# The identity and eight transposes in the rounded 32-bit type, in a hybrid encoder layer

## The chip, the cores and the metric

The kernel runs on one core of a Trainium2 chip. The metric is the device time of one execution in microseconds (us); smaller is better. TensorE (PE) multiplies and transposes, VectorE (DVE), ScalarE (ACT) and GpSimd (POOL) do the rest, and SyncE (SP) issues most loads.

## The reference

One layer of a bidirectional encoder on 1024 tokens of 1024 features, in float32: a gated feed-forward half-step, a mixer of two attention branches, a second half-step and a last norm.

```
h = x + 0.5 * swiglu(rms_norm(x, n1), wg1, wu1, wd1)          # d_ff = 2816
u = rms_norm(h, nm)
qa, ka, va, qb, kb, vb, ga, gb = split(u @ w_in)
ya = neighbourhood_attention_2d(qa, ka, va, rpb)               # 8 heads of 64, 8x16 windows, bias
yb = windowed_gqa_sink(rope(qb), rope(kb), vb, sink)           # 8 query heads, 2 key/value heads,
                                                               # |i - j| <= 128, a sink logit
h = h + (sigmoid(ga) * (ya @ w_a) + sigmoid(gb) * (yb @ w_b)) @ w_out
h = h + 0.5 * swiglu(rms_norm(h, n2), wg2, wu2, wd2)
y = rms_norm(h, nf)
```

The change concerns `vb`, the values of branch B: 1024 tokens by 2 heads of 64.

## The kernel before, in words

All matrix products work on the "rounded" 32-bit type (`F32R` in the code, `fp32r` in the profile). An operand is split into a rounded high part and a low part that holds the rest, and each product is the sum of three matmuls: high by high, high by low, low by high (`mm3`, L149, L153, L155). The feed-forward products and the input projection are arranged as Strassen-like products of half matrices (P1 to P7).

The stages follow one another on TensorE: the first feed-forward half, a transition with the norm, the input projection (`products` with `store_z`), the two attention branches with gates and branch projections as filling work, the output projection, the second feed-forward half.

**The start.** `make_identity` fills `ident`, 128x128, on POOL with a memset (masks.py:197) and an affine select (masks.py:199). The first thing that TensorE does is `keep_busy(28)` (L914 to L919): 28 transposes of the identity whose result nobody reads. Behind them, in TensorE's queue, comes the first stage. Its order is written out by hand, token by token, in `LOADS` and `TABLE`, inside a block in which the order of all five queues is given by the program. `hi:` and `lo:` tokens make the two parts of an operand (L998 and L327 on ACT, L1000 and L334 on DVE), `square:` squares blocks of the input on ACT (L965), `add:` adds them on DVE (L968), `mm:` runs one step of a product, `sum:` adds the squares over the partitions with a matrix of ones (L974), `spread:` turns the resulting factors across the partitions with four transposes (L986), and the `y:` tokens (L1005) apply them. The identity is made outside that block, ahead of it in the program; outside such blocks a scheduler sets the place of an instruction in its engine's queue.

**The values of branch B.** The input projection writes chunk 17, the transposed values (128 features by 1024 tokens), to DRAM. `v_b` (L1153) loads it back to `mix["vr"]`, and `turn_v` (L1158) transposes it in eight blocks of 128x128 with the identity (L1163), four to a PSUM bank; then `split` (L95 on ACT, L98 on DVE) makes the high and low parts from PSUM. Both are hooked into the input projection and run among its products.

The identity also serves the transposes of the transitions (`turned`, L142), of the first stage's `spread` (L986) and of the attention probabilities (`turn`, L1620). The tile `gain` in the constant pool has one buffer, which holds one norm's gains after another, and the ones of the first stage (L926 to L929) before them.

Of the kernel before, what the change touches and what calls it, by code (L numbers as in the profile page):

```python
# [10 lines left out]
F32 = mybir.dt.float32  # L11
F32R = mybir.dt.float32r
# [3 lines left out]
P = 128  # L16
# [15 lines left out]
def f32v(ap):  # L32
    return ap.bitcast(F32)
# [3 lines left out]
def trunk_kernel(ctx, tc, x, xt, n1, wg1, wu1, wd1, nm, win, rpb, sink, wa, wb, wout,  # L37
                 n2, wg2, wu2, wd2, nf, c_rope, c_mask_a, c_mask_b, out):
    nc = tc.nc
# [7 lines left out]
    const = ctx.enter_context(tc.tile_pool(name="const", bufs=1))  # L47
    main = ctx.enter_context(tc.tile_pool(name="main", bufs=1))
# [5 lines left out]
    def nm_(s):  # L54
        uid[0] += 1
        return f"{s}_{uid[0]}"

    ident = const.tile([P, P], F32, name="ident")
    make_identity(nc, ident)
    nhalf4 = const.tile([P, 4], F32, name="nhalf")  # L60
    nc.gpsimd.memset(nhalf4, -0.5)
    nhalf = nhalf4[:, 0:1]
# [17 lines left out]
    def bank(tag):  # L80
        return ps.tile([P, 512], F32, tag=tag, name=nm_(tag))
# [4 lines left out]
    def xs4():  # L86
        return main.tile([P, 1024], F32, tag="xs", bufs=2, name=nm_("xs"))
# [4 lines left out]
    pin = tc.keep_in_program_order  # L92
# [44 lines left out]
    def turned(xs):  # L137
        pts = []
        for half in range(2):
            pt = bank("d")  # L140
            for c in range(4):
                nc.tensor.transpose(pt[:, c * P:(c + 1) * P], xs[:, (half * 4 + c) * P:(half * 4 + c + 1) * P], ident)  # L142
            pts.append(pt.rearrange("p (c t) -> p c t", c=4))
        return pts

# [45 lines left out]
    def rhs(o):  # L191
        return [ar[o][:, k:k + 2, :].rearrange("p a (b t) -> p (a b) t", b=2) for k in (0, 2)]
# [648 lines left out]
    for i in range(NC8 + 2 * len(gates)):  # L841
        n = int(95 - 1.3 * i)
# [71 lines left out]
    def keep_busy(n):  # L914

        b = bank("g")
        for i in range(n):
            k = i % 4 * P
            nc.tensor.transpose(b[:, k:k + P], ident, ident)  # L919

    def first_stage():
        load, _, _, _, pieces, (multiply, finish), hand_over, load_early = hg
# [9 lines left out]
        for token in LOADS.split():  # L932
# [10 lines left out]
            else:  # L943
                k = 2 * (t - 1) + a[1]
# [17 lines left out]
        def do(op, a):  # L962
            if op == "square":
                n, c = int(a[0]), int(a[1])
                nc.scalar.activation(sq[place[4 * (1 - n) + c]], block(c, 0, n), AF.Square, scale=D ** -0.5)  # L965
            elif op == "add":
                d, e = [sq[k] for k in sums[int(a[0])]]
                nc.vector.tensor_tensor(d, d, e, op=ALU.add)  # L968
            elif op == "sum":
                i = int(a[0])  # L970
                if i == 0:
                    mean.append(bank("g"))
                for k in range(4):
                    nc.tensor.matmul(mean[0][:, k * P:(k + 1) * P], sq[3 * i][:, k * P:(k + 1) * P], ones, start=i + k == 0, stop=i == 1,  # L974
                                     skip_group_check=True)
            elif op == "eps":
                i = int(a[0])
                nc.vector.tensor_scalar(st[i][1], st[1][0] if i else mean[0].rearrange("p (k c) -> p k c", c=P)[:, :, 0], EPS, None, op0=ALU.add)
            elif op == "pow":
                i = int(a[0])  # L980
                nc.gpsimd.tensor_tensor(st[i][0], st[i][1], nhalf4, op=ALU.pow)
            elif op == "spread":
                i = int(a[0])
                r[i] = bank("d" if i else "g")
                for k in range(4):
                    nc.tensor.transpose(r[i][:, k * P:(k + 1) * P], st[i][0][:, k:k + 1].to_broadcast([P, P]), ident)  # L986
            elif op == "stat":
                t = int(a[0])
                nc.scalar.activation(toks[:, t - 4], toks[:, t - 4], AF.Square, scale=D ** -0.5,
                                     accum_out=st[1][0][:, t - 4:t - 3])  # L990
            elif op == "keep":
                rms["row"] = main.tile([P, 512], F32, tag="s1", bufs=1, name=nm_("s1"))
                nc.scalar.copy(rms["row"], r[0])
            elif a[0] == "X":
                c = int(a[1])
                h, l = [v[:, c, :] for v in rhs(B21)]
                if op == "hi":
                    nc.scalar.activation(h, block(c, 0, 1), AF.Copy, scale=n1c[:, 4 + c:5 + c])  # L998
                else:
                    nc.vector.scalar_tensor_tensor(out=l, in0=block(c, 0, 1), scalar=n1c[:, 4 + c:5 + c], in1=f32v(h),  # L1000
                                                   op0=ALU.mult, op1=ALU.subtract)
            elif op == "y":
                n, h, c = int(a[0][0]) - 1, int(a[0][1]) - 1, int(a[1])
                d, k = block(c, h, n), 4 * n + c
                nc.vector.scalar_tensor_tensor(out=d, in0=d, scalar=n1c[:, k:k + 1],  # L1005
                                               in1=rms["row"] if (n, h) == (1, 0) else r[h], op0=ALU.mult, op1=ALU.mult)
            elif op == "t":
                c = int(a[1])
                y11, y21, y12, y22 = block(c, 0, 0), block(c, 0, 1), block(c, 1, 0), block(c, 1, 1)
                d, u, v = {"1": (y12, y12, y11), "2": (y22, y22, y12), "3": (y11, y22, y11), "4": (y21, y21, y22)}[a[0]]  # L1010
                nc.vector.tensor_tensor(d, u, v, op=ALU.subtract)
            elif a[0] in RIGHTS:
                c = int(a[1])
                src, g = block(c, *BLOCKS[a[0]]), RIGHTS[a[0]]
                if ar[g].dtype != F32R:
                    new_ar(g)
                h, l = [v[:, c, :] for v in rhs(RIGHTS[a[0]])]
                if op == "hi":
                    nc.scalar.copy(h, src)
                else:  # L1020
                    nc.vector.tensor_tensor(l, src, f32v(h), op=ALU.subtract)
            elif op == "load":
                i, m, half = [int(k) for k in a]
                load(i, m, half, {(0, 0): 4, (0, 1): 5, (1, 0): 6}[m, half])
            else:
                q = int(a[1]), a[0], int(a[2])
                if op == "mm":
                    if q not in mm:
                        mm[q] = multiply(*q)
                    drain(mm[q], 1)  # L1030
# [21 lines left out]
    z_d = dram.tile([GA, T], F32, name="z_d")  # L1052
# [8 lines left out]
    gain = load_gain(nm[0])  # L1061
    mix = {}
# [89 lines left out]

    def v_b():  # L1153
        mix["vb"] = [new_fx(k, F32R).rearrange("p (t d) -> p t d", t=NTT) for k in (0, 1)]
        mix["vr"] = xs4()
        pin(nc.sync.dma_start(mix["vr"], z_d[17 * P:18 * P, :]))

    def turn_v():  # L1158
        r = mix["vr"]
        for n in range(2):  # L1160
            pt = bank("g")
            for i in range(4):
                nc.tensor.transpose(pt[:, i * P:(i + 1) * P], r[:, (4 * n + i) * P:(4 * n + i + 1) * P], ident)  # L1163
            pt = pt.rearrange("p (b s d) -> p b s d", s=2, d=HD)
            for s in range(2):
                v = mix["vb"][s][:, 4 * n:4 * n + 4, :]
                split(v[:, :, :HD], v[:, :, HD:], pt[:, :, s, :])
# [77 lines left out]
    for c in range(5):  # L1245
        n = 14 * (NG - 1) - 6 - 7 * c
# [367 lines left out]
    def turn(un):  # L1614
        nk = un["nk"]
        un["p"] = [ws4()[:, :768].rearrange("p (k s t) -> p k s t", k=3, s=2) for _ in range(2)]
        for s in range(2):
            pt = bank("d")
            for i in range(nk):
                nc.tensor.transpose(pt[:, i * P:(i + 1) * P], un["pr"][s][:, i * P:(i + 1) * P], ident)  # L1620
# [183 lines left out]
    gain = load_gain(n2[0])  # L1804
# [13 lines left out]
    gain = load_gain(nf)  # L1818
# [122 lines left out]
```

## Time and profile before

| | |
|---|---|
| time, median of 3 runs | 1912.86 us (1912.05 to 1912.9) |
| the profiled execution's own time | 1912.05 us |
| its span | 1910.1 us |
| TensorE busy | 1901.1 us, 9020 instructions |
| VectorE, ScalarE, GpSimd busy | 1456.1, 961.3, 244.3 us |
| read from and written to HBM | 244.06 and 121.83 MB, 192 GB/s over the span |
| eight transposes of the values (L1163) | from 810.87 us, 272 ns each |
| 28 transposes of `keep_busy` (L919) | from 1.52 us, 421 ns each |

Rows of a timeline give the start and the length in us, the engine, the line, what is written and read, and in brackets the idle time ahead and what ended it. Matmuls are pipelined: one starts before the one ahead has ended, so the distance of two starts is their price in a stream, and the length of one is longer. Weight loads (PEld) run beside the matmuls.

### The profile page before, as it was taken

To read this page: it belongs to the slowest core of one execution; us is meant where nothing else is said; L and a number is where in the kernel's file an instruction comes from. 1 tells how busy PE (TensorE), PEld (TensorE's weight loads), DVE (VectorE), ACT (ScalarE), POOL (GpSimd) and SP (SyncE) were. 2 spreads that over 40 slices of the span, in tenths; PEclk is the share of its full clock that TensorE was granted. 3 is DMA by queue.
4 is the path that set the end of the run, shared out by engine and by line. 5 is a ranking of instruction groups with operands and counts; after the bars stand their busy time and mean duration, and the time that the engine had idled before them with its cause. 6 is when DMAs were issued, how large, how long until landed. Compare 5 with 4: busy or idle time off the path is not lost.

```text
span 1910.1 us, 26150 instructions
## 1 busy us (share of the span) xinstructions
PE 1901.1 (100%) x9020; PEld 1595.1 (84%) x9020; DVE 1456.1 (76%) x2644; ACT 961.3 (50%) x1876; POOL 244.3 (13%) x453
## 2 busy tenths in 40 slices
PE   9999999999999999999999999999999999999998
PEld 8888888888888888898898888888888888888886
DVE  8988888868957788666888999789665566559664
ACT  7533545544446543444898885274333333344453
POOL 0011232210000112211112300010010001000011
PEclk9999999999999999999999999999999999999999
DMA  7256977887454367855647969653333323492341
GB/s 270 95 188 217 336 273 289 298 293 282 127 166 135 112 206 225 243 192 206 181 123 207 296 227 335 232 195 132 136 111 107 108 89 111 162 357 93 110 139 61
DMA packets 176963, 365.84 MB, mean 192 GB/s; under 512 B 17728, under 2 KB 75968, under 8 KB 176832
## 3 DMA queue, kind: packets, MB, share of 16 engines
q1 hardware_dynamic: 136784, 236.23, 37.6%
q0 software_dynamic: 39184, 126.90, 19.2%
q8 instruction: 71, 1.16, 0.3%
q10 hardware_dynamic: 864, 1.05, 0.2%
q14 instruction: 60, 0.49, 0.1%
HBM read 244.06 MB, written 121.83 MB: 192 GB/s over the span
## 4 chain that ended last, share of the span: by engine, by line
PE 96%; ACT 2%; DVE 1%; DMA 0%; issue 0%; SPq 0%; POOLq 0%; POOL 0%; DVEq 0%
PE g L149 18%; PE g L155 18%; PE g L153 18%; PE d L155 12%; PE d L149 12%; PE d L153 12%; PE d L1620 2%; PE g L1634 1%; PE d L1596 1%; PE d L1597 1%; PE g L1639 1%; PE d L142 1%; ACT fa L1604 0%; ACT ws L95 0%; DMA fx<-in_xt_dram 0%; DVE ws L98 0%
## 5 line engine op out<-in xcount | busy, mean ns | idle before, releaser
L149 PE MATMUL g<-ar,ws 128*128 128x512 f32 x1062 | 407.0, 393 | 0.2
L153 PE MATMUL g<-ar,ws 128*128 128x512 f32 x1062 | 403.8, 390 | 0.0
L155 PE MATMUL g<-ar,ws 128*128 128x512 f32 x1062 | 402.6, 390 | 0.0
L149 PE MATMUL d<-ar,ws 128*128 128x512 f32 x706 | 275.3, 390 | 0.0
L155 PE MATMUL d<-ar,ws 128*128 128x512 f32 x706 | 274.9, 389 | 0.1
L153 PE MATMUL d<-ar,ws 128*128 128x512 f32 x706 | 274.8, 389 | 0.0
L155 PEld LDWEIGHTS g<-ar,ws 128*128 128x128 f32 x1062 | 199.2, 188 | 41.8
L153 PEld LDWEIGHTS g<-ar,ws 128*128 128x128 f32 x1062 | 199.4, 188 | 40.7
L149 PEld LDWEIGHTS g<-ar,ws 128*128 128x128 f32 x1062 | 196.4, 188 | 37.1 <-ACT xs L1331 1.1
L334 DVE TENSOR_TENSOR ws<-raw,ws 128x512 fp32r<-128x512 f32 x216 | 147.6, 689 | 78.5 <-ACT ws L327 77.7
L327 ACT CAST ws<-raw 128x512 fp32r<-128x512 f32 x216 | 132.7, 620 | 143.1 <-PE g L155 61.2
L155 PEld LDWEIGHTS d<-ar,ws 128*128 128x128 f32 x706 | 132.5, 188 | 28.0 <-DVE ws L334 0.5
L153 PEld LDWEIGHTS d<-ar,ws 128*128 128x128 f32 x706 | 132.6, 188 | 27.7 <-DVE ar L1000 0.3
L149 PEld LDWEIGHTS d<-ar,ws 128*128 128x128 f32 x706 | 132.7, 188 | 27.1
L95 ACT CAST ws<-raw 128x512 fp32r<-128x512 f32 x88 | 54.9, 623 | 115.5 <-PE d L155 63.6
L98 DVE TENSOR_TENSOR ws<-raw,ws 128x512 fp32r<-128x512 f32 x88 | 60.5, 688 | 55.2 <-ACT ws L95 55.1
L95 ACT CAST ar<-raw 128x512 fp32r<-128x512 f32 (+1 forms) x80 | 52.1, 654 | 84.4 <-PE g L153 51.5
L446 POOL DMA_DIRECT2D hid<-fx x91 | 49.5, 544 | 343.2 <-DVE fx L506 221.6
L149 PE MATMUL g<-ws,ws 128*128 128x512 f32 x232 | 90.9, 392 | 0.0
L153 PE MATMUL g<-ws,ws 128*128 128x512 f32 x232 | 90.3, 389 | 0.0
L155 PE MATMUL g<-ws,ws 128*128 128x512 f32 x232 | 90.1, 390 | 0.0
L95 ACT CAST ws<-ar 128x512 fp32r<-128x512 f32 x104 | 64.3, 618 | 47.4 <-PE g L155 25.4
(382 smaller groups left out, 3878.7 us busy)
## 6 DMA issues: line engine op xcount, KB each, us to landing
raw<-hid SPq DMA_DIRECT2D x70, 512.0 KB
hid<-fx POOLq DMA_DIRECT2D x91, 256.0 KB, 2.9
ar<-in_ffn_w_down_dram SPq DMA_DIRECT2D x32, 512.0 KB
raw<-in_ffn_w_up_dram SPq DMA_DIRECT2D x31, 512.0 KB
wo_d<-made POOLq DMA_DIRECT2D x28, 512.0 KB, 4.6
raw<-in_ffn_w_gate_dram SPq DMA_DIRECT2D x27, 512.0 KB
hid<-fa POOLq DMA_DIRECT2D x51, 256.0 KB, 2.9
ar<-zs_d POOLq DMA_DIRECT2D x48, 256.0 KB, 9.3
```

The lines of the kernel that those rows point to most:

```text
L95: hi = nc.scalar.copy(dst_hi, src)
L98: (eng or nc.vector).tensor_tensor(dst_lo, src, f32v(dst_hi), op=ALU.subtract)
L142: nc.tensor.transpose(pt[:, c * P:(c + 1) * P], xs[:, (half * 4 + c) * P:(half * 4 + c + 1) * P], ident)
L149: o = nc.tensor.matmul(b, lhs[0], r[0], start=first, stop=False, **kw)
L153: nc.tensor.matmul(b, lhs[0], r[1], start=False, stop=False, **kw)
L155: nc.tensor.matmul(b, lhs[1], r[0], start=False, stop=last, **kw)
L327: nc.scalar.copy(w[0][:, :512], a)
L334: nc.vector.tensor_tensor(w[0][:, 512:], a, f32v(w[0][:, :512]), op=ALU.subtract)
L446: nc.gpsimd.dma_start(hid[PRODUCTS.index(p), i], src)
L1596: nc.tensor.matmul(b[:, :nw], un["q"][s], un["kd"][s][:, k0 * P:k1 * P], start=True, stop=False)
L1597: nc.tensor.matmul(b[:, :nw], un["q"][s], un["kl"][s][:, k0 * P:k1 * P], start=False, stop=True)
L1620: nc.tensor.transpose(pt[:, i * P:(i + 1) * P], un["pr"][s][:, i * P:(i + 1) * P], ident)
```

## The change

`ident` becomes a tile of the rounded type. The plain identity is made in `plain`, a view of the one `gain` buffer, and a copy on VectorE writes `ident` from it. The eight transposes of `turn_v` take the values, the identity and the output as the rounded type; for that the values are loaded to a tile of this type, from the same ring of buffers as before. All other transposes read `ident` as plain 32-bit.

```diff
-    ident = const.tile([P, P], F32, name="ident")
-    make_identity(nc, ident)
+    ident = const.tile([P, P], F32R, name="ident")
+    plain = const.tile([P, 1152], F32, tag="gain", bufs=1, name="plain")[:, :P]
+    make_identity(nc, plain)
+    nc.vector.tensor_copy(ident, plain)
...
-            nc.tensor.transpose(b[:, k:k + P], ident, ident)
+            nc.tensor.transpose(b[:, k:k + P], f32v(ident), f32v(ident))
...
-        mix["vr"] = xs4()
-        pin(nc.sync.dma_start(mix["vr"], z_d[17 * P:18 * P, :]))
+        mix["vr"] = main.tile([P, 1024], F32R, tag="xs", bufs=2, name=nm_("vr"))
+        pin(nc.sync.dma_start(f32v(mix["vr"]), z_d[17 * P:18 * P, :]))
...
-                nc.tensor.transpose(pt[:, i * P:(i + 1) * P], r[:, (4 * n + i) * P:(4 * n + i + 1) * P], ident)
+                nc.tensor.transpose(pt[:, i * P:(i + 1) * P].bitcast(F32R), r[:, (4 * n + i) * P:(4 * n + i + 1) * P], ident)
```

The three other uses of the identity (L142, L986, L1620) get `f32v(ident)` in the same way. Behind the start every line number is 2 higher in the changed kernel.

How the queues stand, first VectorE's at the start of the program. The names are tiles (`ar`, `ws`, `xs`, `fx`, `raw` are work buffers, `n1c` the first norm's gains); in brackets are the engines whose signals an instruction waits for. Before:

```order
L1000 SCALAR_TENSOR_TENSOR ar_80<-fx_77,n1c,ar_80 128x512 [waits DMAHW1_49,DMAHW0_49,Activation_49]
L334 TENSOR_TENSOR ws_169<-raw_103,ws_169 128x512 [waits DMAHW2_49,Activation_49]
L1000 SCALAR_TENSOR_TENSOR ar_80<-fx_77,n1c,ar_80 128x512 [waits DMAHW3_49,Activation_49]
L968 TENSOR_TENSOR xs_133<-xs_133 128x512 [waits Activation_49]
L1000 SCALAR_TENSOR_TENSOR ar_80<-fx_78,n1c,ar_80 128x512 [waits DMAHW4_49,Activation_49]
L1000 SCALAR_TENSOR_TENSOR ar_80<-fx_78,n1c,ar_80 128x512 [waits Activation_49]
L334 TENSOR_TENSOR ws_188<-raw_107,ws_188 128x512 [waits DMAHW5_49,Activation_49]
```

And now:

```order
L1002 SCALAR_TENSOR_TENSOR ar_82<-fx_79,n1c,ar_82 128x512 [waits DMAHW1_49,DMAHW0_49,Activation_49]
L336 TENSOR_TENSOR ws_171<-raw_105,ws_171 128x512 [waits DMAHW2_49,Activation_49]
L1002 SCALAR_TENSOR_TENSOR ar_82<-fx_79,n1c,ar_82 128x512 [waits DMAHW3_49,Activation_49]
L970 TENSOR_TENSOR xs_135<-xs_135 128x512 [waits Activation_49]
L1002 SCALAR_TENSOR_TENSOR ar_82<-fx_80,n1c,ar_82 128x512 [waits DMAHW4_49,Activation_49]
L1002 SCALAR_TENSOR_TENSOR ar_82<-fx_80,n1c,ar_82 128x512 [waits Activation_49]
L61 CAST ident<-plain 128x128 [waits Pool_49]
L336 TENSOR_TENSOR ws_190<-raw_109,ws_190 128x512 [waits DMAHW5_49,Activation_49]
```

The copy of the identity (L61) stands in the seventh place, behind six instructions of the first stage. TensorE's queue at the start, before:

```order
L919 MATMUL g_139<-ident 128x128 [waits Pool_49]
L919 MATMUL g_139<-ident 128x128 x27
L149 MATMUL d_175<-ar_80,ws_169 128x512 [waits Activation_49]
L153 MATMUL d_175<-ar_80,ws_169 128x512 [waits DVE_49]
L155 MATMUL d_175<-ar_80,ws_169 128x512 [waits DVE_49]
```

And now:

```order
L921 MATMUL g_141<-ident 128x128 [waits DVE_49]
L921 MATMUL g_141<-ident 128x128 x27
L151 MATMUL d_177<-ar_82,ws_171 128x512 [waits Activation_49]
L155 MATMUL d_177<-ar_82,ws_171 128x512
L157 MATMUL d_177<-ar_82,ws_171 128x512
```

The first of the 28 transposes waits for VectorE and no longer for POOL; the place of the 28 is the same. On POOL the filling of the ones (L931) now stands behind the affine select and waits for VectorE. The last place is ScalarE's queue around the eight transposes, where `g` are the banks of the turned values, `fx` their high parts and `ws` weights of later products. Before:

```order
L324 CAST ws_6778<-fx_77 128x4x128
L324 CAST ws_6778<-raw_6487 128x4x128
L95 CAST fx_6579<-g_6759 128x4x64
L95 CAST v_6755<-fa 128x8x64
L95 CAST fx_6579<-g_6768 128x4x64
L95 CAST fx_6580<-g_6759 128x4x64
L95 CAST fx_6580<-g_6768 128x4x64
L1116 ACTIVATE fa<-d_6785 128x512
```

And now:

```order
L326 CAST ws_6780<-fx_79 128x4x128
L97 CAST fx_6581<-g_6761 128x4x64
L326 CAST ws_6780<-raw_6489 128x4x128
L97 CAST v_6757<-fa 128x8x64
L97 CAST fx_6581<-g_6770 128x4x64
L97 CAST fx_6582<-g_6761 128x4x64
L1118 ACTIVATE fa<-d_6787 128x512
L97 CAST fx_6582<-g_6770 128x4x64
```

The first copy of turned values moved one place up, the last one place down; VectorE's subtractions that go with them move likewise. Elsewhere all queues stand as before.

More of the change, by code (lines that the diff above doesn't have):

```diff
@@ L141, in turned @@
             for c in range(4):
-                nc.tensor.transpose(pt[:, c * P:(c + 1) * P], xs[:, (half * 4 + c) * P:(half * 4 + c + 1) * P], ident)
+                nc.tensor.transpose(pt[:, c * P:(c + 1) * P], xs[:, (half * 4 + c) * P:(half * 4 + c + 1) * P], f32v(ident))
             pts.append(pt.rearrange("p (c t) -> p c t", c=4))
@@ L985, in do @@
                 for k in range(4):
-                    nc.tensor.transpose(r[i][:, k * P:(k + 1) * P], st[i][0][:, k:k + 1].to_broadcast([P, P]), ident)
+                    nc.tensor.transpose(r[i][:, k * P:(k + 1) * P], st[i][0][:, k:k + 1].to_broadcast([P, P]), f32v(ident))
             elif op == "stat":
@@ L1619, in turn @@
             for i in range(nk):
-                nc.tensor.transpose(pt[:, i * P:(i + 1) * P], un["pr"][s][:, i * P:(i + 1) * P], ident)
+                nc.tensor.transpose(pt[:, i * P:(i + 1) * P], un["pr"][s][:, i * P:(i + 1) * P], f32v(ident))
             if len(un["v"]) == 2:
```

## The prediction

> **What bounds the kernel now.** I read the page's first and fourth part first, then a table of stretches, then the timeline of the first 20 us, because the change touches the identity and the identity is the first thing that TensorE needs.
>
> ```profile
> span 1910.1 us, 26150 instructions
> PE 1901.1 (100%) x9020; PEld 1595.1 (84%) x9020; DVE 1456.1 (76%) x2644; ACT 961.3 (50%) x1876; POOL 244.3 (13%) x453
> PE 96%; ACT 2%; DVE 1%; DMA 0%; issue 0%; SPq 0%; POOLq 0%; POOL 0%; DVEq 0%
> ```
>
> TensorE is busy for 1901.1 of 1910.1 us and holds 96% of the chain that ended last. What makes TensorE start later is therefore not hidden, unless TensorE waits for something else afterwards. Its 9 us without work lie at the two ends:
>
> ```profile
> 0.00:10.00 10.00, 8.47 (x38) 7.77 (x39) 4.25 (x7) 6.79 (x12) 0.89 (x9) 1.00 0.79 265
> 10.00:20.00 10.00, 9.90 (x54) 8.18 (x54) 7.78 (x13) 7.81 (x15) 1.03 (x1) 1.00 1.03 412
> 20.00:30.00 10.00, 10.00 (x46) 8.26 (x45) 9.88 (x18) 8.14 (x16) 0.61 (x1) 1.00 1.03 408
> 1900.00:1910.10 10.10, 3.10 (x14) 2.25 (x12) 2.82 (x6) 3.27 (x9) 1.68 (x5) 0.77 0.43 156
> ```
>
> (The columns after the stretch and its length are busy us and instructions of PE, its weight loads, DVE, ACT and POOL, then granted clock, DMA share and GB/s.) 1.53 us are missing in the first 10 us and 7.00 in the last; everything between is full. So the start is the one place where this change can move the whole program. There the timeline shows:
>
> ```profile
> 1.19 0.29 POOL masks.py:199 TENSOR_SCALAR_AFFINE_SELECT ident<-ident 128x128 f32<-128x128 f32 x1
> 1.52 6.23 PE L919 MATMUL g<-ident 128*128 128x128 f32 x28 [1.52 <-POOL ident masks.py:199]
> 7.41 0.59 PE L149 MATMUL d<-ar,ws 128*128 128x512 f32 x1
> 7.83 0.39 PE L153 MATMUL d<-ar,ws 128*128 128x512 f32 x1
> 8.06 0.40 PE L155 MATMUL d<-ar,ws 128*128 128x512 f32 x1
> 13.03 0.39 PE L155 MATMUL d<-ar,ws 128*128 128x512 f32 x1
> 13.52 2.05 PE L974 MATMUL g<-ones,xs 128*128 128x128 f32 x16
> ```
>
> POOL finishes the identity at 1.19 + 0.29 = 1.48. TensorE starts 28 dummy transposes 0.04 us later, at 1.52, and keeps at them until the first product at 7.41: 5.89 us. The products follow 0.23 us apart (7.83 to 8.06). 24 of them run until 13.03, then the sums of squares start at 13.52. Although TensorE was busy, the chain of waits passes the transposes by:
>
> ```profile
> 2.11 5.57 DMA fx<-in_xt_dram
> 12.77 0.70 DVE xs L968
> 13.52 2.05 PE g L974 x16
> ```
>
> The sums waited for VectorE's additions, which go back to a load that landed at 7.68. The dummy transposes have a little room today: the products could begin later by the time that TensorE lost in waits before 13.52. How much is that? 24 products cost 0.42 for the first (7.41 to 7.83) and 23 times 0.23 for the rest, 5.71 in all, but 13.52 - 7.41 = 6.11 passed. The room is 0.40 us.
>
> **The change part by part.** *The start.* The identity that TensorE reads is now written by one VectorE copy from the plain one. The order of VectorE's queue, shown with the change, does not put this copy first. It stands seventh, behind four multiply-subtracts (L1000 before), one subtraction (L334) and one addition (L968). VectorE takes them in turn, and in the trace they run like this:
>
> ```profile
> 4.87 0.75 DVE L1000 SCALAR_TENSOR_TENSOR ar<-fx,n1c,ar 128x512 fp32r<-128x512 f32 x1 [4.87 <-ACT ar L998]
> 5.53 0.68 DVE L334 TENSOR_TENSOR ws<-raw,ws 128x512 fp32r<-128x512 f32 x1
> 6.67 0.75 DVE L1000 SCALAR_TENSOR_TENSOR ar<-fx,n1c,ar 128x512 fp32r<-128x512 f32 x1 [0.45 <-ACT ar L998]
> 7.33 0.68 DVE L968 TENSOR_TENSOR xs<-xs 128x512 f32<-128x512 f32 x1
> 8.46 1.42 DVE L1000 SCALAR_TENSOR_TENSOR ar<-fx,n1c,ar 128x512 fp32r<-128x512 f32 x2 [0.44 <-ACT ar L998]
> 9.79 0.68 DVE L334 TENSOR_TENSOR ws<-raw,ws 128x512 fp32r<-128x512 f32 x1
> ```
>
> None of the six waits for TensorE, so their times stay: they follow the loads and ScalarE. The copy takes the place in which the last row starts, 9.79. The plain identity is ready by then, since POOL makes it at the very start in either order. How long a copy of 128x128 takes, the trace does not show; the nearest rows on VectorE are one element and 256 elements per partition:
>
> ```profile
> L1600 DVE COPY hs<-nsk 128x1 f32<-128x1 f32 x20 | 2.7, 139 | 5.5 <-DMA zs_d<-hs 4.3 <-ACT hs L1604 1.1
> L1611 DVE TENSOR_SCALAR fa<-fa,rc 128x256 f32<-128x256 f32 x11 | 3.9, 362 | 0.2
> ```
>
> So 0.14 to 0.36; between them, at half of 256 elements, I take 0.25. The copy ends at 10.04, and with the same 0.04 us from the writer's end to TensorE's start the transposes begin at 10.08 instead of 1.52. They stand ahead of every product in TensorE's queue, and their number is unchanged. At the same pace the first product starts at 10.08 + 5.89 = 15.97 and the sums at 15.97 + 5.71 = 21.68, because all that the products and the sums need has been ready since 13.52. Against 13.52 that is **+8.16 us**. (8.56 later at the start, less the room of 0.40.)
>
> The pace of the transposes is the term that I am least sure of:
>
> ```profile
> L919 PE MATMUL g<-ident x28: 421/421/473, 1.5 to 7.3; 128*128 128x128 f32 x28
> L1163 PE MATMUL g<-ident,xs x8: 272/272/273, 811.0 to 811.7; 128*128 128x128 f32 x8
> 810.87 0.90 PEld L1163 LDWEIGHTS g<-ident,xs 128*128 128x128 f32 x8
> 811.74 0.19 PEld L149 LDWEIGHTS d<-ws,ar 128*128 128x128 f32 x1
> ```
>
> At the start they take 421 ns each and follow 5.89 / 28 = 0.21 us apart; the same form takes 272 ns in the middle and follows (811.74 - 810.87) / 8 = 0.109 apart. The start runs at about half pace, and full pace comes with the second product at 7.83, though the granted clock reads 1.00 throughout. If all 28 ran at full pace they would take 3.05 us, 2.84 less; if the half pace lasted 1 us into the products, about 0.5 more. I take no change, since nothing has run on TensorE before them in either kernel. The Trainium skill (TensorE: Matmul & The Clock Gate, Part 1) says that the array runs at half clock until it has been busy through one window of about 3.4 us, and that these windows run freely, not from the kernel's start; the trace agrees as far as full pace came 6.3 us after the first transpose. By that rule full pace could come from 3.4 us on, so that in the best case 16 transposes are slow and 12 fast: 4.6 us, an estimate of 1.3 less.
>
> *After the start.* Who waits for TensorE there? VectorE's normalisation waits for its sums and for the spread of their result:
>
> ```profile
> 15.61 0.16 DVE L978 TENSOR_SCALAR st<-g 128x4 f32<-128x4 f32 x1 [0.34 <-PE g L974]
> 18.74 1.41 DVE L1005 SCALAR_TENSOR_TENSOR fx<-fx,n1c,g 128x512 f32<-128x512 f32 x2 [1.37 <-ACT s L993]
> ```
>
> So VectorE cannot run ahead and then win time: its queue stands at these rows until TensorE has come, and it is 9.88 of 10 us busy right behind. Both engines move as one block. POOL's filling of the ones for the sums now waits for the copy too; it takes 0.2 us and ends near 10.3, 11 us before the sums. It costs nothing; without that cover it would cost 0.2.
>
> *The eight transposes themselves* take 0.87 us now. With rounded operands the trace shows no such row. The nearest are the rounded products with 256 columns around them, 0.12 us apart (the last row is the table's for this stretch):
>
> ```profile
> 810.01 0.28 PE L153 MATMUL d<-ws,ar 128*128 128x256 f32 x1
> 810.13 0.28 PE L155 MATMUL d<-ws,ar 128*128 128x256 f32 x1
> ...
> 800.00:820.00 20.00, 20.00 (x169) 20.00 (x169) 13.36 (x25) 9.39 (x19) 3.19 (x6) 1.00 0.78 238
> ```
>
> Half of that for 128 columns is 8 x 0.06 = 0.48, a gain of 0.4. On the other side I bound them by double the present pace, as in the start rows, a loss of 0.9. I take a gain of **0.2**, nearer to the rounded rows. Their consumers on ScalarE and VectorE change places with a neighbour or two; TensorE is busy for 20.00 of the 20 us around them, and the weights made there are several products ahead, so I cost that at nothing; if it were exposed, one rounding copy would be late, of the length of VectorE's L334 above, 0.68 us.
>
> The load of the values is the same transfer, into the same ring of buffers; the other lines only read the identity as plain again. Cost nil.
>
> Sum: 8.16 - 0.2 = 7.96. The profiled execution took 1912.05, its span and 1.95 around it. 1912.05 + 7.96 = **1920.0 us**. The profiled one is the fastest of the three runs shown, 0.8 below their median, which I keep as room at the top.
>
> **The rivals.** *The delay is paid back.* If the later start let ScalarE, VectorE and the loads get ahead, TensorE's later waits would vanish. What it still waits for:
>
> ```profile
> PEld g L149 <- issue: 1.2, 3, 0.4
> PEld g L149 <- ACT xs L1331: 1.1, 2, 0.6
> PEld d L142 <- issue: 0.5, 2, 0.4
> PEld g L974 <- DVE xs L968: 0.5, 1, 0.5
> PEld g L149 <- ACT ar L95: 0.5, 1, 0.5
> ```
>
> These rows and the eleven below them, none above 0.5, make 7.1 us, of which 0.8 are the start's. If all the rest, 6.3, were won back, the time would be 1920.0 - 6.3 = 1913.7, not slower by what can be told. For it: these waits are real. Against it: none of them is for a load; they are for ScalarE and VectorE, whose inputs come from TensorE's own products, and so move with it. It decides the sign once about 4.2 of the 8.0 us come back.
>
> *The dummy transposes run at full pace*: 2.84 less, 1917.2. For it: nothing fixes when the half pace ends. Against it: 28 of 28 were slow in the profiled start.
>
> *The change does not delay the identity*: if the copy ran when its input was ready, it would end near 1.48 + 0.25, the room of 0.40 would cover it, and only the transposes' 0.2 would be left: 1911.9. Against it stands the order of the queue, which held row for row in the trace of before.
>
> *The rounded transposes are what counts*: at twice the pace they cost 0.9, at half of it they bring 0.4; neither can be told from no change, with or without the late start.
>
> **How the numbers follow.** The late start at about its full price: 0.80, 1920.0. The late start with a warm-up that gets fast early: 0.10, about 1917 to 1919. Paid back: 0.06, 1913.7. No delay at all: 0.03, 1911.9. For a gain no mechanism has a price above 0.4 us: 0.01. About 0.2%, 3.8 us, is what a measurement of this kernel can tell from no change: slower 0.90, same 0.09, faster 0.01. The range runs from 1917.0 (the fast warm-up) to 1921.8: 0.8 for the median, 0.5 for a longer half pace and 0.5 of the 1.1 by which the transposes could miss my value.
>
> **What would show it.** Right: the 28 transposes of the changed kernel start near 10.1, released by VectorE's copy of the identity; the first product stands near 16.0 and the sums of squares near 21.7, with no wait ahead of them; PE's idle time in the first 10 us is all of it; from 30 us on every row stands about 8 us later, up to the end. Wrong: transposes that start near 1.8 (the copy ran early); a first product before 14 (the pace); rows that come closer to their old times somewhere after 30 us, with waits of TensorE gone there (paid back). The eight transposes' own pace can be read between their first weight load and the next product's.

## The result, and the profile after

The changed kernel takes 1921.99 us (median of six executions, 1918.72 to 1928.61), the one before, run beside it, 1912.47 (1911.93 to 1912.90). The ratio is 1.0053, interval [1.0042, 1.0063]: slower by 9.5 us between the medians (10.1 by the ratio). The forecast was 1920.0, with a range of 1917.0 to 1921.8. The direction held; the median lies 0.2 us above the range. Two executions of 3.9 and 4.0 ms, one of the changed kernel and one of the kernel before, both beside later experiments, are left out of all figures below; their cause is not known. The profiled execution is the fastest of the six, 1918.72, and it lacks a loss that the profile of a slower one, further down, shows. Its page begins:

```profile
span 1916.3 us, 26151 instructions
PE 1898.9 (99%) x9020; PEld 1593.2 (83%) x9020; DVE 1455.3 (76%) x2645; ACT 960.7 (50%) x1876; POOL 244.5 (13%) x453
```

TensorE is busy 2.2 us less than before (1901.1), but the span has grown by 6.2. The added time is idle time, and the timeline shows where: at the start. These are rows of the changed kernel's timeline from its first copy to its last matmul (line numbers are 2 higher than before):

```profile
9.78 0.22 DVE L61 CAST ident<-plain 128x128 fp32r<-128x128 f32 x1
10.05 4.78 PE L921 MATMUL g<-ident 128*128 128x128 f32 x28 [10.05 <-DVE ident L61]
14.59 0.47 PE L151 MATMUL d<-ar,ws 128*128 128x512 f32 x1
20.15 1.95 PE L976 MATMUL g<-ones,xs 128*128 128x128 f32 x16
23.99 0.60 PE L988 MATMUL g<-ident,st 128*128 128x128 f32 x4
...
817.38 0.28 PE L157 MATMUL d<-ws,ar 128*128 128x256 f32 x1
817.50 0.79 PE L1165 MATMUL g<-ident,vr 128*128 128x128 f32 x8
818.13 0.35 PE L151 MATMUL d<-ws,ar 128*128 128x256 f32 x1
...
1908.96 0.39 PE L157 MATMUL g<-ar 128*128 128x512 f32 x1
```

And those rows of the kernel before that the prediction does not show:

```profile
17.48 0.60 PE L986 MATMUL g<-ident,st 128*128 128x128 f32 x4
...
810.86 0.28 PE L155 MATMUL d<-ws,ar 128*128 128x256 f32 x1
810.98 1.03 PE L1163 MATMUL g<-ident,xs 128*128 128x128 f32 x8
811.77 0.36 PE L149 MATMUL d<-ws,ar 128*128 128x256 f32 x1
...
1902.71 0.39 PE L155 MATMUL g<-ar 128*128 128x512 f32 x1
```

Read them as differences, place by place. The 28 transposes start 8.53 us later (10.05 against 1.52), the sums 6.63 later (20.15 against 13.52), the spread 6.51 later, the product ahead of the eight transposes 6.52 later, the last matmul 6.25 later. Between the start and the values nothing is won or lost. Around the eight transposes, from the start of the product ahead to that of the product behind, 0.75 us pass where 0.91 passed before: 0.16 won. So in this execution the change costs what the start costs, less 0.16.

The start costs less than forecast because the transposes were quicker: 4.54 us from the first one to the first product (10.05 to 14.59), against 5.89 before. The view of that line gives the spread of their durations:

```profile
L921 PE MATMUL g<-ident x28: 272/369/473, 10.1 to 14.6; 128*128 128x128 f32 x28
```

Before, the least was 421 ns; now some take 272, the full pace of the middle of the program. The half pace ended while the transposes were still running.

### The profile page after: what moved, and what is told of

Its sections match the earlier page's. It is cut to its first block, busy times and chain, and to the rows that moved or that the text cites. A ratio compares the mean times of both kernels' runs of the same rounds, so it can differ in the third digit from the quotient of the medians.

```text
span 1916.3 us, 26151 instructions
## 1 busy us (share of the span) xinstructions
PE 1898.9 (99%) x9020; PEld 1593.2 (83%) x9020; DVE 1455.3 (76%) x2645; ACT 960.7 (50%) x1876; POOL 244.5 (13%) x453
## 4 chain that ended last, share of the span: by engine, by line
PE 95%; ACT 2%; DVE 2%; issue 0%; DMA 0%; POOL 0%; POOLq 0%; DVEq 0%; ACTq 0%
PE g L151 17%; PE g L157 17%; PE g L155 17%; PE d L157 12%; PE d L151 12%; PE d L155 12%; PE d L1622 2%; PE g L1636 1%; PE d L1598 1%; PE d L1599 1%; PE g L1641 1%; PE d L144 1%; ACT fa L1606 0%; ACT ws L97 0%; DVE ws L100 0%
```

## The experiments

The median lies 3.3 us above the profiled execution, and the spread of the six, 10 us, is ten times that of the kernel before. One theory said that the late start is all, with a warm-up of varying length as its spread. Its rivals were that the rounded type or the moved queues cost something too, and, once the first traces had been read, that a second wait appears in most executions. The first four runs shared one chip and one set of runs of the kernel before, as did the next four and the last four.

### The transposes read the plain identity

```diff
-            nc.tensor.transpose(b[:, k:k + P], f32v(ident), f32v(ident))
+            nc.tensor.transpose(b[:, k:k + P], plain, plain)
```

Everything else of the change stays; only the 28 dummy transposes no longer wait for the copy.

> The changed kernel, but the 28 transposes at the start read the plain identity, which POOL has ready at 1.33 us in the changed kernel's profile; the copy to the rounded type stays seventh in VectorE's queue and the eight transposes stay rounded. If the late start is the cause: transposes from about 1.4 us, sums of squares near 13.5 as before, time 1912.0 to 1912.6, no slower than before by what can be told, and runs within 1 us of one another as before. If the rounded type or the copy itself costs the time: 1919 or more, as in the changed kernel.

Measured: median 1916.24 of ten (1911.99 to 1921.94), ratio 1.0017 [1.0007, 1.0027]. The profiled execution took 1912.54, with the start back in its place:

```profile
1.39 6.22 PE L921 MATMUL g<-plain 128*128 128x128 f32 x28 [1.39 <-POOL plain masks.py:199]
13.79 2.02 PE L976 MATMUL g<-ones,xs 128*128 128x128 f32 x16 [0.32 <-DVE xs L970]
...
1099.05 0.42 DVE L1566 TENSOR_TENSOR fa<-g,s 64x256 f32<-64x256 f32 x1 [0.43 <-DMA y_d<-fa]
```

The start fell as expected, and the best executions equal the best of the kernel before. The times did not: 1912.0 to 1912.6 within 1 us was expected, but seven of ten lie above 1914.5, and the late start is not there to explain them. The last row gave the lead: VectorE waited 0.43 us for a store, a wait that the profile of the kernel before does not show.

### The copy alone, nothing rounded

```diff
-    make_identity(nc, ident)
+    plain = const.tile([P, 1152], F32, tag="gain", bufs=1, name="plain")[:, :P]
+    make_identity(nc, plain)
+    nc.vector.tensor_copy(ident, plain)
```

This is the kernel before with this edit alone; `ident` stays plain and the values stay as they were.

> The kernel before with one edit: the identity is made in the same plain tile and copied by VectorE to ident, but ident stays plain 32-bit and so do the eight transposes. The copy stands seventh in VectorE's queue as in the changed kernel. If the late start is the cause: start of the 28 transposes near 10.05 us, time 1919 to 1929 with the same spread as the changed kernel, 0.2 us above it. If the rounded type is the cause: 1912.5.

Measured: 1923.66 (1920.47 to 1926.49), ratio 1.0053 [1.0040, 1.0066], the ratio of the whole change. The profiled execution has the late start and a larger wait of the same kind as above:

```profile
10.44 5.05 PE L921 MATMUL g<-ident 128*128 128x128 f32 x28 [10.44 <-DVE ident L61]
20.82 1.95 PE L976 MATMUL g<-ones,xs 128*128 128x128 f32 x16
...
1109.38 0.42 DVE L1566 TENSOR_TENSOR fa<-g,s 64x256 f32<-64x256 f32 x1 [3.69 <-DMA y_d<-fa]
```

So the damage needs no rounded type. Of the span's 12.2 us (1922.3 against 1910.1) the sums carry 7.30 (20.82 against 13.52), and 4.9 are lost elsewhere.

### Sixty transposes in place of 28

```diff
-        keep_busy(28)
+        keep_busy(60)
```

> The changed kernel with 60 instead of 28 transposes at the start. The six runs of the changed kernel lie between 1918.7 and 1928.6 us, those of before within 1 us. If that spread comes from the moment at which TensorE reaches its full pace, with real products running slowly until then in the long runs, 60 transposes (6.5 us at full pace, 12.5 at half) cover it: all products run 0.23 us apart, the runs stay within 2 us of one another, at 10.05 plus 8.2 to 9.9 for the transposes, so 1922 to 1925. If the spread comes from later in the program: it stays near 10 us, and the median is near 1926.

Measured: 1923.54 (1921.87 to 1923.99), ratio 1.0051 [1.0038, 1.0064]. In the profiled execution the transposes run from 9.60 to the first product at 17.66, 8.06 us, and the sums start at 23.23, 9.71 late; the span is 9.3 longer. 60 at the full pace of 0.109 would take 6.54, so some 15 of them ran at half pace and the rest at full pace: the warm-up was over well inside the transposes, and what stood behind that point was work ahead of the products that passed on in full. In this execution VectorE had no wait for the store, and in the four executions the time varies by 2 us only. Median and spread are those that were expected if the warm-up made the spread; but that theory does not hold, as the next trace and the stores on ScalarE's queue show. Why four executions in a row vary so little is not known.

### The changed kernel again

No edit; the question was what a profile of a slower execution shows.

> The changed kernel unchanged, for its spread and a second trace. Late start alone with a pace that varies: first product between 14.0 and 16.5 us and time between 1918 and 1921. If something else adds to it, times above 1922 come again, and a trace of such a run shows where: products more than 0.23 us apart at the start, or waits of TensorE later that the first trace does not have.

Measured: five executions of 1919.99 to 1927.28, their median 1925.13, ratio 1.0056 [1.0043, 1.0069]. The profiled one took 1925.9, and its timeline shows both losses:

```profile
10.45 6.05 PE L921 MATMUL g<-ident 128*128 128x128 f32 x28 [10.45 <-DVE ident L61]
16.25 0.48 PE L151 MATMUL d<-ar,ws 128*128 128x512 f32 x1
21.79 1.95 PE L976 MATMUL g<-ones,xs 128*128 128x128 f32 x16
...
1088.55 0.32 SPq L1452 DMA_DIRECT2D ws<-wb_d  x1
1088.96 0.38 SPq L1448 DMA_DIRECT2D masks<-g_d  x1
1090.58 0.59 SPq L1568 DMA_DIRECT2D y_d<-fa  x1
...
1110.33 0.42 DVE L1566 TENSOR_TENSOR fa<-g,s 64x256 f32<-64x256 f32 x1 [4.11 <-DMA y_d<-fa]
1111.28 0.44 PE L1598 MATMUL d<-ar 128*128 128x384 f32 x1 [3.77 <-DVE nmx L1603]
```

The start is the forecast's almost to the row: 5.80 us of transposes at half pace, the first product at 16.25, the sums at 21.79. That is 8.27 late, while the span (1923.6) is 13.5 longer; 5.4 come from the second place (13.5 less 8.27, plus the 0.16 won).

There, near 1110 us, branch A's results of one head pair after the other go into one buffer, columns 3072 to 4096 of `fa`. VectorE writes them (L1566) and SyncE stores them to DRAM (L1568), half a buffer at a time. The next head pair's first write to a half has to wait until its store has read it. In this execution the store was issued at 1090.58, and it was over 19.65 us later, as the chain of waits shows:

```profile
1090.58 19.65 DMA y_d<-fa
```

VectorE stood for 4.11 us with the softmax of the next scores behind it in its queue (`nmx`, L1603), and TensorE, which the last row shows waiting for that, for 3.77. In the kernel before, the same store and the write that needs its place are these:

```profile
1082.63 0.59 SPq L1566 DMA_DIRECT2D y_d<-fa  x1
...
1098.20 0.41 DVE L1564 TENSOR_TENSOR fa<-g,s 64x256 f32<-64x256 f32 x1
```

The store has 15.57 us there, and it was enough, since the second row has no wait. In the first profile of the changed kernel the distance is 15.56 (1088.91 to 1104.47), with no wait either. The store in the plain-warm run above needed 16.06 (issued at 1082.99) and cost 0.43. So the store has little room to spare in either kernel. The table of stretches of the kernel before shows how busy the transfers are there:

```profile
1040.00:1120.00 80.00, 79.78 (x490) 70.31 (x489) 72.98 (x226) 70.75 (x185) 23.22 (x40) 1.00 1.04 293
```

The DMA share is 1.04: by this measure the engines that move data are busy for all of the 80 us. In the rows of SyncE's queue above, two loads of 512 KB each (`ws`, `masks`) were issued within 2.1 us ahead of the store.

A wait of this length has a tail of its own. The tables of stretches, of the first profile of the changed kernel:

```profile
1100.00:1120.00 20.00, 20.00 (x127) 17.63 (x126) 18.47 (x61) 17.42 (x47) 3.08 (x5) 1.00 0.94 289
```

and of this one:

```profile
1100.00:1120.00 20.00, 16.23 (x89) 14.12 (x89) 13.35 (x43) 13.08 (x35) 4.15 (x6) 0.91 1.05 293
```

TensorE's busy time falls by 3.77, the wait, and the granted clock (the last column but two) falls from 1.00 to 0.91. A stretch of 0.09 x 20 / 0.5 = 3.6 us at half clock gives this, a loss of 1.8 at most. 3.77 + 1.8 = 5.6, and 5.4 were lost. The Trainium skill (TensorE: Matmul & The Clock Gate, the table in "Why this matters for your kernels") says that one idle window, 3.413 us by its Part 1, brings the half clock back. The row agrees with one such window: an estimate from that figure gives 1 - 3.413 x 0.5 / 20 = 0.915.

### The stores on ScalarE's queue, in three kernels

If the queue in which the store stands behind the loads makes it late, then on another queue it should not be. The edit, in the kernel before, in the changed kernel, and in the changed kernel with transposes that read the plain identity:

```diff
-                            nc.sync.dma_start(y_d[512 + hp * P:512 + (hp + 1) * P, cols].rearrange("(s p) t -> p s t", s=2), both)
+                            nc.scalar.dma_start(y_d[512 + hp * P:512 + (hp + 1) * P, cols].rearrange("(s p) t -> p s t", s=2), both)
```

The kernel before with it:

> The kernel before, with the six stores of branch A's result from its one buffer issued on ScalarE's queue instead of SyncE's. In the traces of the second look VectorE waited 3.7 and 4.1 us at 1110 us for such a store, which stood behind 1 MB of other loads on SyncE's queue and landed 19.7 us after its issue; 15.6 us are free. If these stores make the spread: all runs within 1.5 us, median 1912.0 to 1913. If not: single runs of 1915 and above as before has them.

The changed kernel with it:

> The changed kernel with the same edit. If the late start costs 6 to 8 us and the rest of the loss is the late store: 1918.5 to 1921, all runs within 2.5 us (the pace of the 28 transposes), no wait for a store and no stretch at half clock near 1110 us. If the rest has another cause: the median stays at 1922 to 1925 with a spread of 6 and more.

The changed kernel with it and with plain transposes at the start:

> The changed kernel with the 28 transposes on the plain identity and the stores on ScalarE's queue. If the late start and the late store are all that the change costs: 1911.6 to 1913, within 1.5 us, level with or 0.2 below the kernel before with the same stores. If the runs between 1915 and 1922 of the kernel without the store edit have another cause: they come again.

Measured, in us:

| kernel, stores on ScalarE's queue | median | executions | lowest to highest | ratio to the kernel before |
|---|---|---|---|---|
| before | 1913.62 | 10 | 1912.93 to 1914.15 | 0.9999 [0.9990, 1.0009] |
| changed | 1920.87 | 5 | 1919.83 to 1921.45 | 1.0039 [1.0026, 1.0052] |
| changed, identity not waited for | 1913.40 | 10 | 1912.74 to 1913.80 | 1.0001 [0.9992, 1.0010] |

The spread collapses to 1.1 to 1.6 us in all three, as was expected, with the medians of the first and the last 0.6 and 0.4 above what was expected. So the late store made the spread of the changed kernel: 9.9 and 7.3 us in its two sets, 1.6 now. For the kernel before the same is likely and less firm, since 5 of 26 executions beside it were above 1914.5 and 0 of 10 are now. The profile of the changed kernel with this edit has the late start, no wait for a store, and a full clock:

```profile
10.71 5.20 PE L921 MATMUL g<-ident 128*128 128x128 f32 x28 [10.71 <-DVE ident L61]
21.23 1.95 PE L976 MATMUL g<-ones,xs 128*128 128x128 f32 x16
...
1089.92 0.61 ACTq L1568 DMA_DIRECT2D y_d<-fa  x1
...
1108.36 0.41 DVE L1566 TENSOR_TENSOR fa<-g,s 64x256 f32<-64x256 f32 x1
...
1100.00:1200.00 100.00, 99.97 (x536) 85.05 (x535) 92.83 (x231) 71.10 (x161) 8.38 (x14) 1.00 0.83 284
```

The edit does more than change the queue: VectorE's, ScalarE's and SyncE's instructions in this stage come in another order than before, and the store's room has grown to 18.44 us (1089.92 to 1108.36), and to 18.77 and 18.66 in the other two profiles. Four of the six late stores in these traces took longer than that, 19.15 us and more, so the room alone would not have hidden them; but no run separates the queue from the room.

These three kernels give the prices without the late store. The late start costs 1920.87 - 1913.40 = 7.47 us. All else in the change is worth 1913.40 - 1913.62 = -0.22, which is the size of the 0.16 seen at the eight transposes and too small to be told by times alone. The change as a whole, without the late store, costs 7.25. As it stands it costs 9.5, so at the median about 2.3 us are left for the late store; that is a remainder, and in the second set of the changed kernel it is 5.1 (1925.13 - 1912.74 - 7.25). In the profiled slower executions it was 4.9 and 5.4. The Trainium skill (DMA: Bandwidth & Descriptors, Queues, rings and completion order) says that SP and ACT each have a ring of their own on the same 16 engines, that a ring is consumed in order, and that an engine turns from ring to ring by packets. The three rows fit this, in that the same store on the other queue was nowhere late; since its room grew as well, they do not show it.

### No dummy transposes

```diff
-        keep_busy(28)
+        keep_busy(0)
```

> The changed kernel without any of the 28 transposes at the start, the copy still seventh in VectorE's queue. Only the transposes need the identity, so if their place ahead of the products is what makes the copy's lateness cost time: products from about 6.3 us, at half pace until full pace comes, sums between 14 and 17 us, 4 to 7 earlier than in the changed kernel: 1913 to 1916, plus the same late stores later. If the copy's lateness holds the products in some other way: sums still near 20 us, 1918 and above.

Measured: 1915.60 (1911.79 to 1920.64), ratio 1.0008 [0.9996, 1.0021]. The first product starts at 5.79 and the sums at 14.35, within what was expected and 0.83 later than before, though the copy of the identity stands where it stood: among the start's instructions the dummy transposes alone need it so early. The profiled execution, 1920.64, is another case of the late store, the longest wait of these profiles:

```profile
1104.41 0.42 DVE L1566 TENSOR_TENSOR fa<-g,s 64x256 f32<-64x256 f32 x1 [5.66 <-DMA y_d<-fa]
```

Of the 8.2 us by which its span exceeds that of before, the start has 0.83; so one late store can cost about 7 us, with the slower clock behind it.

### The copy on time, in two ways

First the changed kernel with the copy on GpSimd, right behind the affine select that makes the plain identity:

```diff
-    nc.vector.tensor_copy(ident, plain)
+    nc.gpsimd.tensor_copy(ident, plain)
```

> The changed kernel with the copy of the identity on GpSimd's queue, where it stands right behind the affine select, instead of VectorE's. If the place of the copy in VectorE's queue is what makes the change slow: transposes at the start from about 1.7 us, sums near 13.6, best runs 1911.8 to 1912.5; the late store near 1110 us may still add 2 to 9 us in some runs, as it does in the kernel before. If a copy ahead of the transposes is slow wherever it stands: 1918 and above in all runs.

Then the copy-alone kernel, nothing rounded, with the 28 transposes on `plain`:

```diff
-            nc.tensor.transpose(b[:, k:k + P], ident, ident)
+            nc.tensor.transpose(b[:, k:k + P], plain, plain)
```

> The kernel before with the plain tile and the copy on VectorE, the identity and the eight transposes plain, and the 28 transposes on the plain tile, so nothing starts late and nothing is rounded. It asks why runs between 1915 and 1922 are frequent in the changed kernel with a start on time (7 of 10) and rare in the kernel before (7 of 27). If the rounded transposes and the changed order behind them make the store late more often: spread as before, median 1912.5 to 1913. If any small shift of the start does: as frequent as there, median 1915 to 1917.

Measured: 1915.74 (1912.49 to 1920.54), ratio 1.0010 [0.9999, 1.0021]; and 1914.80 (1913.38 to 1921.44), ratio 1.0009 [0.9997, 1.0021]. Both start on time (transposes at 1.74 and 1.38), and both have the wide spread. The first falls as expected for the copy's place being the cause; the second comes close to the branch in which any small shift makes the store late (1915 to 1917), and not to the other. The profile of the first shows it:

```profile
1.74 5.13 PE L921 MATMUL g<-ident 128*128 128x128 f32 x28 [1.74 <-POOL ident L61]
...
1101.98 0.42 DVE L1566 TENSOR_TENSOR fa<-g,s 64x256 f32<-64x256 f32 x1 [3.52 <-DMA y_d<-fa]
```

The second has a wait of 1.97 at the same place. Since it rounds nothing and its transposes start on time, the late store needs neither the rounded type nor the late start. Over 1914.5 us lie 15 of 80 executions of the kernel before, taken over all sets, and 25 of 40 of the four builds whose products start nearly in time and whose store is where it was (plain transposes, none, and these two); in each of the three sets the share is higher in these builds (7 of 10 against 3 of 17, 6 of 10 against 5 of 26, 12 of 20 against 7 of 31). No profile of the kernel before shows a late store; that its slow executions are of this kind is inferred. Why they come more often in the changed builds, no run here shows.

### A smaller store, earlier

The store goes after every second unit instead of every fourth, half as large, so that a place has seven units of time instead of five before it is written again:

```diff
-                        if j in (3, 7):
-                            nc.sync.dma_start(y_d[512 + hp * P:512 + (hp + 1) * P, cols].rearrange("(s p) t -> p s t", s=2), both)
+                        if j % 2:
+                            nc.sync.dma_start(y_d[512 + hp * P:512 + (hp + 1) * P, (j - 1) * P:(j + 1) * P].rearrange("(s p) t -> p s t", s=2),
+                                              both[:, :, (j % 4 - 1) * P:(j % 4 + 1) * P])
```

In the kernel before:

> The kernel before, with branch A's result stored after every second unit instead of after every fourth, so that each store has the time of seven units instead of five before VectorE writes its place again. If the late store is what spreads the kernel before: all runs 1911.5 to 1913, none at 1915 and above. If more and smaller stores cost more than they save: above 1913.5.

In the changed kernel with transposes on the plain identity:

> The changed kernel with the 28 transposes on the plain identity and the stores in pairs. If the late start and the late store are all that stood in the way of the eight rounded transposes: 1911.4 to 1912.6, 0.2 us below the kernel before with the same stores, and faster than both kernels in the median. If not: runs of 1915 and above.

Measured: 1912.76 (1912.15 to 1916.38), ratio 0.9998 [0.9989, 1.0007]; and 1913.82 (1912.44 to 1919.00), ratio 1.0002 [0.9991, 1.0013]. Both miss what was expected if the late store were all: the highest are 1916.38 and 1919.00. Over 1914.5 lie three of ten in each. For the changed build these are fewer than the seven of ten of the plain-warm run; for the kernel before, beside 7 of 31, they are not. Neither beats the kernel before by what can be told, and whether the room helps, ten executions do not show. Neither profile has a wait for the store; in that of the kernel before TensorE waits 0.94 us for a load of weights instead (`ws<-wb_d`, at 1112.74). On ScalarE's queue none of 25 executions was late, at a price of 0.6 us (1913.62 against 1913.00, the median of before in that set).

## Why the prediction was right or wrong

**The copy's place** was right. Forecast: the copy at 9.79 for 0.25 us and the transposes at 10.08. Measured: 9.78, 0.22 and 10.05. In the other profiled executions with the late copy the transposes start at 9.60 to 10.71. The order of VectorE's queue, laid over the times of before, gave the mechanism; that it hit the first execution to 0.03 us is luck, since the others lie up to 0.6 away.

**The pace of the transposes** was the uncertain term, and 5.89 us was the upper end. 28 of them took 4.54, 4.80, 4.95 and 5.80 in the four profiled executions that start late. The first profile, 1918.72, lies between the likeliest case (1920.0) and the rival with a quick warm-up (1917.2), which had 0.10. The best case that the prediction worked out from the Trainium skill (TensorE: Matmul & The Clock Gate, Part 1) was 4.6 us (16 x 0.21 + 12 x 0.109 is 4.7). The 4.54 of the first execution is a little under it: some 15 transposes, about 3.1 us, ran at half pace ((4.54 - 28 x 0.109) / 0.10). Behind the transposes, from product to sums, 5.56 passed where 5.71 was forecast.

**The late start as a whole** was forecast at +8.16, and it measured 6.63, 7.30, 7.71 and 8.27 at the sums of these four against the 13.52 of before, and 7.47 as a difference of medians. (In the two other profiles of the kernel before, with moved or smaller stores, the sums start at 14.04 and 13.83, so single profiles tell this to half a microsecond.) The term was too large by 0.7, for the pace of the transposes, and within what the range allowed.

**The eight transposes** were forecast at -0.2 and measured -0.16 around their place in the trace. The order of VectorE's and ScalarE's queues near them, and the ones on POOL, cost nothing that can be seen: from the sums to the values the delay stays within 0.11 us.

**What failed** is the step behind the start, which the prediction put at nothing: "Both engines move as one block", and with it the sentence of the rival, "none of them is for a load". I looked at the waits that TensorE already had and asked which of them could shrink. I did not look for a wait that was not there yet. A buffer with one place, a store with 15.57 us to leave it, and a DMA share of 1.04 in that stretch were in the profile of before. With the stores on ScalarE's queue the change costs 7.25, and the changed kernel's 1920.87 lies inside the range; as it stands it costs 9.5, and the difference lifted the median over the range's top. The late store cost 4.9 and 5.4 us in the two profiled executions with a late start that have it, and nothing in the two that do not (the first profile and that of the sixty). That the shift of 8 us itself makes the store late is not shown: builds that start in time have it too. In numbers: the forecast added 7.96 to 1912.05; the measured sum is 1912.47 + 7.25 + 2.27 = 1921.99, where 2.27 is what is left over. The errors of the terms, 0.7 too much at the start and 2.3 too little behind it, go against each other, and that 1920.0 came as close as it did is luck.

**The rivals.** Nothing was paid back: the last matmul was 6.25 late in the first profile, after 6.51 at the spread and 0.16 won at the transposes, 0.10 unexplained. That the change does not delay the identity fell with the first row. That the rounded transposes count fell with the run in which nothing is rounded and the ratio is the same.

**What stays open.** Why executions above 1914.5 are 25 of 40 in builds that start in time and 15 of 80 in the kernel before. The moment of the store's issue does not tell the cases apart: issued at 1082.99 it took 16.06 us, at 1083.11 it took 21.30. What stands ahead of it in SyncE's queue does. Two loads of the attention bias, 192 KB each, go ahead of the store; in the kernel before and in the trace with the 4.11 us wait they are these:

```profile
1076.22 1.47 SPq L1288 DMA_DIRECT2D fa<-bm_d  x2
...
1086.08 0.85 SPq L1290 DMA_DIRECT2D fa<-bm_d  x2
```

They are issued 6.41 and 4.50 us ahead of the store. Over the nine profiles that have this store as it was, the three without a wait show 5.99 to 6.56 us and the six with one 5.45 down to 4.29, and the store took longer in nearly that order (16.06 at 5.45, 21.30 at 4.29). The bias loads came this close ahead of the store where SyncE's queue had waited for another store, `g_d<-xs` from GpSimd: 0 to 0.5 us in the first three and in the plain-warm run, 1.2 to 2.2 in the other five. In two of the profiles with the stores on ScalarE's queue SyncE waited 1.3 and 1.7 us there, and nothing was late. No run changed this wait, so it is a lead and not a cause that is shown, and what holds up that other store is open.

## What to carry to other kernels

An instruction that is put outside a hand-ordered block goes where the scheduler puts it; read its place in the queue, and if the first instruction of the bottleneck engine waits for it, the wait is the price. A warm-up that needs no real data should read a tile that is ready first: the same change with its dummy transposes on the plain tile, and the stores on ScalarE's queue, costs nothing that can be told (1.0001 [0.9992, 1.0010]). And before a shift is called harmless, look for one-place buffers behind stores in stretches where the DMA share is at 1: their room, here 15.57 us, is as much a term as a wait that the profile shows.

## What the runs showed of the hardware

The half pace at the start ends at no fixed place. The same 28 transposes took 4.54 to 5.89 us over these profiles, though the granted clock reads 1.00 in that stretch in all of them; the pace of the rows shows it, the clock column does not.

TensorE does not always pay for a wait with its clock. TensorE's own waits at the late store were 3.35 us in the copy-alone run and 3.77 in the changed kernel's second profile, both with a granted clock of 0.91 over the 20 us from 1100, and 5.31 in the run without transposes, with 0.83. The one of 3.17 us, in the run with the copy on GpSimd, left the clock at 1.00:

```profile
1100.00:1120.00 20.00, 17.08 (x107) 15.29 (x108) 16.86 (x55) 15.35 (x39) 1.10 (x2) 1.00 0.85 286
```

There the span grew by 3.4 us over before (1913.5 against 1910.1), of which the sums show 0.38 (13.90 against 13.52), so about the wait alone was lost.

A store of 256 KB that takes under 15.57 us in one execution took 16.06, 17.60, 19.15, 19.33, 19.65 and 21.30 in others, each worked out from its issue to the end of VectorE's wait, or, for the one of 19.65, read from the chain.
